# Pinning the last tiles' top-k behind the sums of the down products, and summing one-hots in one operation

## The chip, the cores and the metric

The kernel runs on one core of a Trainium2 chip. A core has engines that each work through a queue of their own in order: TensorE (PE; PEld is its loading of weights), VectorE (DVE), ScalarE (ACT), GpSimd (POOL), and SyncE (SP), which here only issues DMA transfers. The metric is the device time of one execution in microseconds (us).

## The reference

One layer over 1024 tokens of width 1024, in two halves. The first is a causal convolution beside an RWKV-7 state recurrence, then an output projection and a layer norm. The second, which the change touches, is a product-key retrieval over 128 x 128 = 16384 experts of a single neuron:

```
s1 = q[..., :128] . k1 ; s2 = q[..., 128:] . k2        # 8 heads, 128 keys each
v1, i1 = top_k(s1, 16) ; v2, i2 = top_k(s2, 16)
cand = v1[:, None] + v2[None, :]                       # 256 sums a head
sc, ci = top_k(cand, 16)
experts = i1[ci // 16] * 128 + i2[ci % 16]
gates = softmax(sc)
y2[t] = sum over k of gelu(h[t] . U[e_k]) * gate_k * V[e_k]   # 128 experts a token
x = layer_norm(alpha * x + gate2 * y2)
```

## The kernel before

The tokens are eight tiles of 128. Tiles 0 to 4 are computed densely: a matrix of gates over all 16384 experts is built for each (`gate_matrix`), and the expert stage then multiplies with all of U and V. Tiles 5 to 7 are gathered: for each of 128 choices a token, GpSimd fetches a row of U by an indirect DMA (L1098), VectorE multiplies and sums it (L1106), and then the same with V (L1113). `side` holds these three gathers one after the other, and `gather_to` takes them forward so that they end with the dense work.

The expert stage runs over 32 groups of four blocks of 128 experts. For each block the up products come first (L1178, tile `mg`, two halves of 320 tokens, 24 matmuls each, so 192 in a group). ScalarE applies gelu (L1180), VectorE multiplies with the gates (L1182), ScalarE rounds to `ah` (L1183) and VectorE takes the rest, `al` (L1184). Then come the down products (L1212, tile `md`, three banks): ten in a group, one for each tile of tokens and half of the width, 12 matmuls each. VectorE adds each to `y_acc` (L1217); in group 0 ScalarE copies it instead. The weights come as 512 KB transfers into three raw buffers, ScalarE rounds them and GpSimd takes the rest (L1143).

The choice of experts is made earlier, beside the recurrence and the projections, for tiles 0 to 5: `best16` finds the 16 largest of 128 scores or of 72 candidates, and `choose` turns their positions into two indices by one-hots (compare, L914; multiply with the indices, L917; three halvings by adds, L920; a last add, L922) and makes the softmax. There the multiply and adds are GpSimd's (`E` is `G`). For tiles 6 and 7 the scores are stored, and `choose_late` does this in the expert stage, two heads at a time, with VectorE for all of it (`E` is `V`; its tiles have names that begin with l: `lscore`, `lvi`, `lcand`, `ltkf`, `loh`). I call this the late work. Both functions are generators, and a step is what stands between two yields: 72 steps a tile. One is taken at every third step of the gathers (`LATE`).

The instructions are written in this order, and a scheduler then orders them for each engine: of those whose inputs it reckons to be ready, an engine gets the one that was written first. So an instruction that is ready early can stand well ahead of its place in the text.

Of the kernel before, what the change touches and what calls it, by code (L numbers as in the profile page):

```python
# [16 lines left out]
OP = mybir.AluOpType  # L17
AX = mybir.AxisListType
# [41 lines left out]
NPAGE = 31  # L60
TSLOW = 2
TGATE = 12
LATE = 3
CBUF = 4
GB = 3
ABUF = 6
# [13 lines left out]
def layer_kernel(ctx, tc, x, cols, c_row, cond_w, w_in, w2a2, g2, w_out, ln_rows, wq, keys, peer_u, peer_ut, peer_v, peer_vt, out):  # L80
# [785 lines left out]
    def choose(tt, val, idx, h0, nh, nb, new, E):  # L866

        n = nh * TOPK
        sh3 = [128, nh, TOPK]
        quad = lambda nm, dt=F32: new(nm, dt, 4 * n).rearrange("p (q h r) -> p q h r", q=4, h=nh)  # L870
        qf, qg, qu = quad("tkf"), quad("tkg"), quad("tku", U32)
        fp, m1, m2, m3 = (qf[:, i] for i in range(4))
        top, shf, fo = qg[:, 0], qg[:, 1], (qg[:, 2], qg[:, 3])
        pos = qu[:, 0]
        shi, qi_, ri_ = (qu[:, i].bitcast(I32) for i in (1, 2, 3))
        for hh in range(0, nh, nb):
            hs = slice(hh, hh + nb)
            cand = new("cand", F32, nb * NCAND).rearrange("p (h c) -> p h c", h=nb)
            o = 0
            for i, m, w in REGIONS:  # L880
                V.tensor_add(cand[:, :, o:o + m * w].rearrange("p h (a b) -> p h a b", b=w),
                             val[:, hs, 0, i:i + m][:, :, :, None].to_broadcast([128, nb, m, w]),
                             val[:, hs, 1, 0:w][:, :, None, :].to_broadcast([128, nb, m, w]))
                o += m * w
            for h in range(hh, hh + nb):
                best16(top[:, h], pos[:, h], cand[:, h - hh, :])
                yield

        A.activation(fp, pos, AF.Copy)
        V.tensor_scalar(m1, fp, 32.0, None, op0=OP.is_ge)  # L890
        V.tensor_scalar(m2, fp, 48.0, None, op0=OP.is_ge)
        V.tensor_scalar(m3, fp, 64.0, None, op0=OP.is_ge)
        V.tensor_add(shf, m1, m2)
        V.scalar_tensor_tensor(shf, m3, 2.0, shf, op0=OP.mult, op1=OP.add)
        V.tensor_scalar(shi, shf, -1.0, 4.0, op0=OP.mult, op1=OP.add)
        V.tensor_tensor(qi_, pos.bitcast(I32), shi, op=OP.logical_shift_right)
        V.tensor_tensor(ri_, qi_, shi, op=OP.logical_shift_left)

        V.scalar_tensor_tensor(m1, m2, 3.0, m1, op0=OP.mult, op1=OP.add)
        V.scalar_tensor_tensor(m1, m3, 24.0, m1, op0=OP.mult, op1=OP.add)  # L900
        qb = new("tkb", BF, 8 * n).rearrange("p (q h r) -> p q h r", q=8, h=nh)
        isel, jsel = qb[:, 0], qb[:, 1]
        V.scalar_tensor_tensor(isel, m1, -2.0, qi_, op0=OP.mult, op1=OP.add)
        V.tensor_sub(jsel, fp, ri_)
        yield
        put = lambda w, t: ld(sel_d[tt][w][:, h0 * TOPK:h0 * TOPK + n], t.rearrange("p h r -> p (h r)"))
        for half, sel in ((0, isel), (1, jsel)):
            ib = qb[:, 2 + half]
            A.activation(ib, idx[:, :, half, :], AF.Copy)
            for hh in range(0, nh, nb):  # L910
                hs = slice(hh, hh + nb)
                oh = new("oh", BF, nb * TOPK * TOPK).rearrange("p (h q r) -> p h q r", h=nb, q=TOPK)
                sh4 = [128, nb, TOPK, TOPK]
                V.tensor_tensor(oh, iota_q[:, None].to_broadcast(sh4), sel[:, hs, None, :].to_broadcast(sh4),  # L914
                                op=OP.is_equal)
                yield
                E.tensor_mul(oh, oh, ib[:, hs, :, None].to_broadcast(sh4))  # L917
                yield
                for w in (8, 4, 2):
                    E.tensor_add(oh[:, :, 0:w], oh[:, :, 0:w], oh[:, :, w:2 * w])  # L920
                    yield
                E.tensor_add(fo[half][:, hs], oh[:, :, 0], oh[:, :, 1])  # L922
            put(half, fo[half])
        mx = small.tile([128, NH], F32, name="mx")[:, :nh]
        V.tensor_copy(mx, top[:, :, 0])
        V.tensor_sub(top, top, mx[:, :, None].to_broadcast(sh3))
        A.activation(top, top, AF.Exp)
        sm = small.tile([128, NH], F32, name="sm")[:, :nh]
        V.tensor_reduce(sm, top, axis=AX.X, op=OP.add)
        V.reciprocal(sm, sm)  # L930
        V.tensor_mul(top, top, sm[:, :, None].to_broadcast(sh3))
        put(2, top)
        if tt in DT:
            gates.append(gate_matrix(tt))
        yield
# [187 lines left out]
    done = [0]  # L1123

    def gather_to(frac):

        while side and done[0] < frac * n_side:
            step(side)
            done[0] += 1
            if late and done[0] % LATE == 0:  # L1130
                next(late[min(late)], None)

    NBLK = [slice(a_, a_ + NW) for a_ in range(0, ND, NW)]
    NT = ND // 128
# [25 lines left out]
    for g in range(32):  # L1160
# [38 lines left out]
        for half in range(2):  # L1199
# [3 lines left out]
            for t in range(NT):  # L1203
# [10 lines left out]
                if g == 0:  # L1214
                    A.activation(ya, p, AF.Copy)
                else:
                    V.tensor_add(ya, p, ya)  # L1217
                gather_to((g + 0.5 + (NT * half + t) / (4 * NT)) / 31)
                if g == 31 and half == 1:

# [54 lines left out]
```

## Time and profile before

| | |
|---|---|
| time, median of 3 runs (lowest, highest) | 3313.77 us (3313.57, 3319.34) |
| the profiled execution | 3316.05 us, span 3314.3 us |
| TensorE busy | 3040.8 us, 92% |
| VectorE busy | 2570.2 us, 78% |
| GpSimd busy | 1838.2 us, 55% |
| ScalarE busy | 1212.7 us, 37% |
| first up product (L1178) | at 1431.5 us |
| mean granted clock of TensorE | 0.949 |

The span runs from the first to the last instruction of the profiled execution; the busy times are shares of it, averaged over stages with quite different limits. The expert stage is its second half, from 1431.5 us on. Times of instructions are from the start of the span.

### The profile page before, as it was taken

What the parts mean: (1) busy time and instruction counts of PE and PEld (TensorE: products, weight loads), DVE (VectorE), ACT (ScalarE), POOL (GpSimd) and SP (SyncE); (2) the same over time, 40 slices, a digit from 0 to 9 for tenths busy, and PEclk for the clock granted to TensorE, in tenths of its full rate; (3) what the DMA queues carried; (4) which work ended last, traced back from release to release, by engine and by line L of the source; (5) the groups of instructions that cost most, each with busy time, mean ns of one, the idle gap of its engine ahead of it and who ended that gap; (6) DMA issues with size and microseconds to landing.
All of it is one profiled execution on the core that took longest, in us unless ns stands there. A gap on an engine that the chain in (4) does not pass through costs nothing.

```text
span 3314.3 us, 54838 instructions
## 1 busy us (share of the span) xinstructions
PE 3040.8 (92%) x20400; PEld 2639.3 (80%) x20400; DVE 2570.2 (78%) x5636; ACT 1212.7 (37%) x2358; POOL 1838.2 (55%) x1448
## 2 busy tenths in 40 slices
PE   6968999999897886889899999999999999999996
PEld 4735766678786776878778899999999989898985
DVE  6389565757788889569999977777787867777877
ACT  5552443353444565643223232323232323232323
POOL 2400112233345548446676687778787868777772
PEclk9978999889799887999999999999999999999998
DMA  7885555557576876888788899999999989999994
GB/s 302 292 264 173 159 161 160 178 191 272 169 247 212 300 255 211 262 280 305 267 291 312 302 337 344 337 341 337 337 337 345 335 318 339 346 329 350 331 344 155
DMA packets 403292, 922.31 MB, mean 278 GB/s; under 512 B 80800, under 2 KB 213328, under 8 KB 381008
## 3 DMA queue, kind: packets, MB, share of 16 engines
q1 hardware_dynamic: 210192, 474.16, 41.0%
q0 software_dynamic: 110592, 402.70, 33.5%
q10 hardware_dynamic: 82240, 41.94, 4.4%
q8 instruction: 160, 2.62, 0.3%
q14 instruction: 108, 0.88, 0.1%
HBM read 788.64 MB, written 130.05 MB: 277 GB/s over the span
## 4 chain that ended last, share of the span: by engine, by line
PE 61%; DVE 25%; DMA 4%; POOL 3%; issue 3%; ACT 3%; SPq 0%; DVEq 0%; POOLq 0%; ACTq 0%
PE md L1212 21%; PE mg L1178 21%; PE mm L183 11%; DVE grow L1106 4%; DVE cacc L459 2%; PE mgate L974 2%; PE mm L467 1%; DVE cw L249 1%; DVE oa L962 1%; DVE ob L966 1%; DMA xt<-x 1%; POOL oh L920 1%; PE bank L638 1%; DVE yacc L1217 1%; DVE loh L920 1%
## 5 line engine op out<-in xcount | busy, mean ns | idle before, releaser
L1178 PE MATMUL mg<-h2h,uhi 128*128 128x320 f32 x2048 | 637.0, 311 | 12.9 <-DVE al L1184 12.9
L1178 PE MATMUL mg<-h2l,uhi 128*128 128x320 f32 x2048 | 635.6, 310 | 0.0
L1178 PE MATMUL mg<-h2h,ulo 128*128 128x320 f32 x2048 | 635.5, 310 | 0.0
L1212 PE MATMUL md<-vhi,ah 128*128 128x512 f32 x1280 | 495.2, 393 | 31.3 <-ACT ah L1183 29.0
L1113 DVE SCALAR_TENSOR_TENSOR gy<-grow,gz,gy 128x1024 f32<-128x1024 f32 x381 | 488.6, 1282 | 29.6 <-DMA grow<-peer_v,eid 27.5
L1212 PE MATMUL md<-vhi,al 128*128 128x512 f32 x1280 | 500.8, 392 | 8.2 <-DVE al L1184 8.2
L1098 POOL DMA_INDIRECT grow<-peer_u,eid x384 | 364.3, 949 | 248.7 <-DVE grow L1106 110.2
L1212 PE MATMUL md<-vlo,ah 128*128 128x512 f32 x1280 | 498.3, 391 | 0.0
L1106 DVE SCALAR_TENSOR_TENSOR grow<-grow,gh 128x1024 f32<-128x1024 f32 x384 | 460.6, 1211 | 17.8 <-DMA grow<-peer_u,eid 17.8
L1098 POOL DMA_INDIRECT grow<-peer_v,eid x384 | 361.6, 942 | 190.5 <-DVE gy L1113 106.6
L1178 PEld LDWEIGHTS mg<-h2h,uhi 128*128 128x128 f32 x2048 | 387.2, 189 | 22.8 <-DVE al L1184 17.4
L1178 PEld LDWEIGHTS mg<-h2l,uhi 128*128 128x128 f32 x2048 | 387.2, 189 | 5.1
L1178 PEld LDWEIGHTS mg<-h2h,ulo 128*128 128x128 f32 x2048 | 387.4, 189 | 3.1
L1217 DVE TENSOR_TENSOR yacc<-md,yacc 128x512 f32<-128x512 f32 x310 | 211.4, 687 | 158.0 <-PE md L1212 157.2
L1143 POOL TENSOR_TENSOR vlo<-vraw,vhi 128x1024 fp32r<-128x1024 f32 x128 | 308.9, 2413 | 27.2 <-ACT vhi L1141 24.9
L1143 POOL TENSOR_TENSOR ulo<-uraw,uhi 128x1024 fp32r<-128x1024 f32 x128 | 309.3, 2417 | 24.7 <-ACT uhi L1141 22.7
L1212 PEld LDWEIGHTS md<-vhi,ah 128*128 128x128 f32 x1280 | 240.6, 189 | 82.6 <-ACT ah L1183 33.5
L1212 PEld LDWEIGHTS md<-vhi,al 128*128 128x128 f32 x1280 | 241.5, 189 | 55.5 <-DVE al L1184 10.8
L1212 PEld LDWEIGHTS md<-vlo,ah 128*128 128x128 f32 x1280 | 241.4, 189 | 49.1
L1141 ACT ACTIVATE vhi<-vraw 128x1024 fp32r<-128x1024 f32 x128 | 135.1, 1055 | 393.5 <-DMA vraw<-peer_vt 386.1
L968 POOL TENSOR_TENSOR ob<-ob,selt 128x384 f32<-128x384 f32 x160 | 147.6, 925 | 219.7 <-DVE ob L966 154.7
L974 PE MATMUL mgate<-oa,ob 128*128 128x128 f32 x1280 | 194.4, 305 | 57.2 <-POOL ob L968 51.5
(390 smaller groups left out, 6012.9 us busy)
## 6 DMA issues: line engine op xcount, KB each, us to landing
uraw<-peer_ut SPq DMA_DIRECT2D x128, 512.0 KB, 6.7
vraw<-peer_vt SPq DMA_DIRECT2D x128, 512.0 KB, 5.6
wsplit<-split_wq SPq DMA_DIRECT2D x48, 1024.0 KB, 7.0
G_d<-stage ACTq DMA_DIRECT2D x20, 2048.0 KB, 11.2
gmat<-G_d SPq DMA_DIRECT2D x32, 1280.0 KB, 9.1
cw<-cond_w SPq DMA_DIRECT2D x48, 512.0 KB, 5.5
wsplit<-split_w_out SPq DMA_DIRECT2D x24, 1024.0 KB, 7.6
split_w_in<-wsplit SPq DMA_DIRECT2D x22, 1024.0 KB, 5.0
```

Source lines behind the costliest of these rows:

```text
L183: T.matmul(pt, l[:, k, :], r[k], start=i == 0, stop=i == 3 * KD - 1)
L459: V.scalar_tensor_tensor(a, win(i), wk(i), a, op0=OP.mult, op1=OP.add)
L968: G.tensor_mul(ob[:, :3], ob[:, :3], gt[:, ts.start:ts.start + 3, None].to_broadcast([128, 3, 128]))
L974: T.matmul(pt[:, t, :], ob[:, t, :], oa[:, t, :], start=True, stop=True)
L1098: G.indirect_dma_start(out=r, out_offset=None, in_=peer_u if k < 128 else peer_v, in_offset=bass.IndirectOffsetOnAxis(ap=eid[:, k % 128:k ...
L1106: V.scalar_tensor_tensor(r, r, 1.0, ht, op0=OP.mult, op1=OP.mult, accum_out=z[:, i:i + 1])
L1113: V.scalar_tensor_tensor(y, r, z[:, i - 128:i - 127], y, op0=OP.mult, op1=OP.add)
L1141: A.activation(hi, raw, AF.Copy)
L1143: G.tensor_sub(lo, raw, hi.bitcast(F32))
L1178: T.matmul(p, l[:, k, :], r[k][:, bs], start=i == 0, stop=i == 3 * KD - 1)
L1212: T.matmul(p, l[:, ts], r[:, e % 2, :], start=e == 0 and q == 0, stop=e == 3 and q == 2)
L1217: V.tensor_add(ya, p, ya)
```

## The change

The one-hots of the late work are summed by one reduction over a transposed view in place of four adds. `choose` gets three more yields, for all tiles. The late work is no longer advanced by the gathers' steps but by the sums of the down products from group 1 on, one step for each sum. While a step is written, each of its VectorE instructions gets an edge to that sum: VectorE's order must have it behind the sum. (Instructions of other engines get no such edge, and no wait is added, since both are on one engine.) A tile has 60 steps now.

```
-LATE = 3
...
         V.tensor_scalar(m3, fp, 64.0, None, op0=OP.is_ge)
+        yield
         V.tensor_add(shf, m1, m2)
...
         V.tensor_scalar(shi, shf, -1.0, 4.0, op0=OP.mult, op1=OP.add)
+        yield
         V.tensor_tensor(qi_, pos.bitcast(I32), shi, op=OP.logical_shift_right)
...
         V.scalar_tensor_tensor(m1, m3, 24.0, m1, op0=OP.mult, op1=OP.add)
+        yield
         qb = new("tkb", BF, 8 * n).rearrange("p (q h r) -> p q h r", q=8, h=nh)
...
                 E.tensor_mul(oh, oh, ib[:, hs, :, None].to_broadcast(sh4))
                 yield
+                if E is V:
+                    V.tensor_reduce(fo[half][:, hs], oh.rearrange("p h q r -> p h r q"), axis=AX.X, op=OP.add)
+                    continue
                 for w in (8, 4, 2):
...
             done[0] += 1
-            if late and done[0] % LATE == 0:
-                next(late[min(late)], None)
...
-                    V.tensor_add(ya, p, ya)
+                    ins = V.tensor_add(ya, p, ya)
+                    if late:
+
+                        with tc.issue_after(ins.ins):
+                            t_ = min(late)
+                            if next(late[t_], late) is late:
+                                late.pop(t_)
```

Two places in VectorE's order. The first is the start of the expert stage; `mg<-mg,gmat` is the multiply by the gates. Before:

```order
L751 MAX lvi<-lscore 128x8 x4
L752 MAX_INDEX lvi<-lvi,lscore 128x8 x4
L881 TENSOR_TENSOR lcand<-lvi 128x2x16 x2
L753 MATCH_REPLACE lscore<-lvi,lscore 128x128 x4
L754 MAX lvi<-lscore 128x8 x4
L755 MAX_INDEX lvi<-lvi,lscore 128x8 x3
L881 TENSOR_TENSOR lcand<-lvi 128x2x8
L755 MAX_INDEX lvi<-lvi,lscore 128x8
L1182 TENSOR_TENSOR mg<-mg,gmat 128x320 x3
```

The same place in the changed kernel (its line numbers are 3 to 5 higher here: L1111 is the gathers' L1106, L1185 the multiply, L1187 `al`):

```order
L1091 SCALAR_TENSOR_TENSOR eid<-gsel_14669,gsel_14671 128x128
L1111 SCALAR_TENSOR_TENSOR grow,gz<-grow,gh 128x1024 x5
L1185 TENSOR_TENSOR mg<-mg,gmat 128x320 x3
L1187 TENSOR_TENSOR al<-mg,ah 128x320 x3
L1111 SCALAR_TENSOR_TENSOR grow,gz<-grow,gh 128x1024 x2
```

The first scores' top-k stood ahead of the first multiply; now five gathers do.

The second place is one-hots of tile 6, in the middle of the up products of an early group. Before:

```order
L914 TENSOR_TENSOR loh<-iota_q,ltkb 128x512
L1106 SCALAR_TENSOR_TENSOR grow,gz<-grow,gh 128x1024 x2
L917 TENSOR_TENSOR loh<-loh,ltkb 128x512
L1184 TENSOR_TENSOR al<-mg,ah 128x320
L1106 SCALAR_TENSOR_TENSOR grow,gz<-grow,gh 128x1024
L1182 TENSOR_TENSOR mg<-mg,gmat 128x320
L920 TENSOR_TENSOR loh<-loh 128x2x128
L1106 SCALAR_TENSOR_TENSOR grow,gz<-grow,gh 128x1024
L1182 TENSOR_TENSOR mg<-mg,gmat 128x320
L920 TENSOR_TENSOR loh<-loh 128x2x64
L1184 TENSOR_TENSOR al<-mg,ah 128x320
```

One-hots of tile 6 in the changed kernel (L1220 is the sum of a down product, L916 the compare, L919 the multiply, L922 the reduction):

```order
L1220 TENSOR_TENSOR yacc<-md,yacc 128x512
L916 TENSOR_TENSOR loh<-iota_q,ltkb 128x512
L1220 TENSOR_TENSOR yacc<-md,yacc 128x512
L919 TENSOR_TENSOR loh<-loh,ltkb 128x512
L1111 SCALAR_TENSOR_TENSOR grow,gz<-grow,gh 128x1024 x2
L1220 TENSOR_TENSOR yacc<-md,yacc 128x512
L922 TENSOR_REDUCE ltkg<-loh 128x32
L1111 SCALAR_TENSOR_TENSOR grow,gz<-grow,gh 128x1024
L916 TENSOR_TENSOR loh<-iota_q,ltkb 128x512
```

They stood among the multiplies and `al` of the up products; now each step stands behind a sum, and in this group no late instruction stands between multiplies and `al`.

## Rows read from the trace of the kernel before

**Rows 1.** VectorE's busy share (tenths) in 40 slices of the span, from the page.

```profile
DVE  6389565757788889569999977777787867777877
```

**Rows 2.** Stretches of the expert stage: length, busy us (instructions) of PE PEld DVE ACT POOL, PEclk, DMA, GB/s.

```profile
1431.53:1485.76 54.23, 41.60 (x262) 39.71 (x261) 36.69 (x127) 19.28 (x32) 24.65 (x19) 0.87 0.80 279
1485.76:1931.10 445.34, 407.39 (x2192) 361.92 (x2191) 436.85 (x1026) 131.79 (x225) 302.50 (x231) 0.98 0.85 297
1986.53:2541.33 554.80, 554.80 (x3124) 507.05 (x3122) 432.68 (x650) 152.39 (x247) 427.59 (x328) 1.00 0.93 339
```

**Rows 3.** The same for the up products (L1178): PE, then PEld.

```profile
1485.76:1931.10 445.34, 215.72 (x1344) 207.49 (x1344) 0.98 0.85 297
1986.53:2541.33 554.80, 289.99 (x1921) 285.28 (x1920) 1.00 0.93 339
```

**Rows 4.** Who TensorE waited for, groups 1 to 7: us in total, times, longest.

```profile
PE md L1212 <- ACT ah L1183: 15.0, 10, 3.0
PE mg L1178 <- DVE al L1184: 12.9, 10, 2.5
```

**Rows 5.** Groups 0 to 7, VectorE's lines L1106, L1113, L1182, L1184, L1217, in this order.

```profile
1431.53:1931.10 499.57, 155.14 (x256) 0.97 0.84 295
1431.53:1931.10 499.57, 68.53 (x54) 0.97 0.84 295
1431.53:1931.10 499.57, 31.08 (x64) 0.97 0.84 295
1431.53:1931.10 499.57, 30.56 (x64) 0.97 0.84 295
1431.53:1931.10 499.57, 41.97 (x62) 0.97 0.84 295
```

**Rows 6.** VectorE in time, 1458 us: start us, us, instruction.

```profile
1458.19 1.27 DVE L1182 TENSOR_TENSOR mg<-mg,gmat 128x320 f32<-128x320 f32 x3
```

**Rows 7.** Late lines, groups 0 to 7, by shape: busy us, mean ns | idle before.

```profile
L920 DVE TENSOR_TENSOR loh<-loh 128x256 bf16<-128x256 bf16 x16 | 9.4, 590 | 0.0
L920 DVE TENSOR_TENSOR loh<-loh 128x128 bf16<-128x128 bf16 x16 | 11.8, 736 | 0.0
L920 DVE TENSOR_TENSOR loh<-loh 128x64 bf16<-128x64 bf16 x16 | 9.2, 577 | 0.1
L922 DVE TENSOR_TENSOR ltkg<-loh 128x32 f32<-128x32 bf16 x16 | 4.8, 297 | 0.1
L925 DVE COPY mx<-ltkg 128x2 f32<-128x2 f32 x8 | 10.4, 1295 | 0.0
L929 DVE TENSOR_REDUCE sm<-ltkg 128x2 f32<-128x32 f32 x8 | 1.4, 177 | 0.5 <-ACT ltkg L927 0.5
```

**Rows 8.** A reduction of 512 values elsewhere in the kernel, same view.

```profile
L713 DVE TENSOR_REDUCE gs<-yt 128x8 f32<-128x512 f32 x8 | 5.4, 674 | 0.0
```

**Rows 9.** VectorE in time, 1607 us.

```profile
1607.48 2.77 DVE L914 TENSOR_TENSOR loh<-iota_q,ltkb 128x512 bf16<-128x512 bf16 x1
```

**Rows 10.** GpSimd in time, 1607 us.

```profile
1607.54 2.43 POOL L1143 TENSOR_TENSOR ulo<-uraw,uhi 128x1024 fp32r<-128x1024 f32 x1
```

**Rows 11.** GpSimd's subtractions (L1143) in two stretches: length, POOL busy.

```profile
1485.76:1931.10 445.34, 137.80 (x58) 0.98 0.85 297
1986.53:2541.33 554.80, 193.57 (x81) 1.00 0.93 339
```

**Rows 12.** Who SyncE's queue waited for, 1450 to 1900 us.

```profile
SPq L906 <- DVE ltkg L922: 70.1, 12, 11.9
```

**Rows 13.** GpSimd in time, the fifth gather.

```profile
1452.35 0.94 POOL L1098 DMA_INDIRECT grow<-peer_u,eid  x1 [0.30 <-issue]
```

**Rows 14.** DMA issues, 1446 to 1463 us: count, median us to landing.

```profile
grow<-peer_u,eid POOLq DMA_INDIRECT x6, 10.3
```

**Rows 15.** The stretch before the expert stage, columns as in rows 2.

```profile
815.00:1431.53 616.53, 519.00 (x4767) 479.03 (x4765) 486.15 (x1621) 327.14 (x779) 312.52 (x316) 0.90 0.72 239
```

**Rows 16.** The down products (L1212) of groups 9 to 18: PE, then PEld.

```profile
1986.53:2541.33 554.80, 281.76 (x1203) 223.71 (x1202) 1.00 0.93 339
```

## Prediction

> **What bounds the kernel now.** I read the table of 40 slices first. VectorE's digits [rows 1] are 9 in the slices just after the middle, where the expert stage begins, and 7 and 8 from there on: the engine is full for some 450 us and then no longer. Next came the table by stretches, cut at the first up product of groups 0, 1, 8, 9 and 19 of the 32 groups [rows 2]. That these cuts hold whole groups is seen from the up products alone [rows 3]: 1344 are 7 x 192, and 1920 are 10 x 192. So groups 1 to 7 take 445.3 us, 63.6 each, and groups 9 to 18 take 554.8 us, 55.5 each. In the second stretch TensorE is busy for all of it, VectorE for 432.7 us (43.3 a group), and nothing waits. In the first VectorE is busy for 436.9 of 445.3 us (98.1%) while TensorE stands for 38 us. Had the first seven groups run at 55.5 they would take 388.4; the excess is 57.0 us. It is more than the 38 us of standing still: the granted clock is 0.98 on average there, that is the upper of its two levels (2.4 GHz) but for short pieces at the lower (1.2 GHz) after TensorE stood, against 1.00, and ends of matmuls are modelled.
>
> The longest waits of TensorE in those groups [rows 4] are for the copy ah, which follows VectorE's multiply by the gates (15.0 us), and for VectorE's own al (12.9). So in groups 1 to 7 VectorE is the bound, and TensorE from group 9 on. What the first has and the second has not are the late steps, the top-k and choice of tiles 6 and 7. In the 500 us of groups 0 to 7 VectorE is busy 36.7 + 436.9 = 473.5 us [rows 2]; the gathers' two lines, the multiply, al and the sums are 155.1 + 68.5 + 31.1 + 30.6 + 42.0 = 327.3 [rows 5]. The rest, 146 us, is late work, and more than that, since an instruction starts before its predecessor ends: three multiplies back to back took 1.27 us [rows 6], three single ones would be 3 x 0.486 = 1.46, so 0.09 less for each that follows. With half of the 500 instructions so packed that is 22 us, and late work 168. Between 146 and 168 I take 160, the nearer to full packing, since the engine hardly stood.
>
> **The change, part by part.** *The one-hot sums.* Three halvings and a last add, 64 instructions in all, go; their busy times are 11.8 + 9.4 + 9.2 + 4.8 = 35.2 us [rows 7]. Sixteen reductions come, 512 bf16 values each. The trace has reductions of 512 f32 values at 674 ns [rows 8]; 16 x 0.674 = 10.8 us. The difference is 24.4, less 2 for 48 packed starts: 22 us saved. The bounds: a reduction in strides of bf16 is not shown. At the least it costs what 32 elements cost, 0.18 us [rows 7], and saves 30; at the most what the four adds cost, 2.2 us, and saves nothing. I take 674 ns, the row with the same count.
>
> Why adds of 64 elements take 577 ns is seen in a pair of rows: a compare on VectorE ran from 1607.48 for 2.77 us, just behind GpSimd's subtraction of the low weights, 1607.54 for 2.43 us [rows 9, 10]. The copy of 2 elements takes 1295 ns on average for the same reason, while the small reductions stay at 177 ns [rows 7]. The Trainium skill says in "GPSIMD Engine Reference", Key points, that GpSimd's SBUF interfaces are shared with VectorE instructions that have two SBUF inputs or run in a two-port mode; a reduction is neither, so by that page the 16 never wait and 10.8 us stands, where being held as the copy is, some 1.1 us each, would make it 29. The trace agrees as far as those eight small reductions go.
>
> Against this change speaks "VectorE: DVE Perf Modes" of the Trainium skill, Rules for kernel authors: it calls `tensor_reduce` the slowest operation of VectorE, to be restructured on a hot path, and its tier table gives 16-bit adds twice the rate. By it the swap saves nothing; that is the second rival below, worked out there from rows.
>
> *The other late work* keeps its instructions. The subtractions that hold it fill 137.8 of 445.3 us now (31%) and 193.6 of 554.8 (35%) where groups are short [rows 11], so what is held grows by about an eighth. With some 55 us of the late work held, a third of it, that is +7; the bounds are 0 and +12. Late work after the change: 160 - 22 + 7 = 145 us.
>
> *The pinning.* A tile now has 4 x 15 = 60 steps and one call that finds the end, so two tiles take 122 sums, ten in each group from group 1 on: 12.2 groups, where before they were done by group 7 and partly in group 0. Each group carries 145 / 12.2 = 11.9 us. VectorE then needs 43.3 + 11.9 = 55.2 us, about TensorE's 55.5. With the 98.1% to which it was filled before, that is 56.2 a group, 0.7 over, or 9 us in all. Two engines that are both full also make each other wait. No stretch shows such a balance; bounds are 0 and 2 us a group, I take 0.6, 7 us.
>
> The pinned instructions stand behind a sum that itself waits for TensorE, and behind them on VectorE are the next gather and the next sum. Between the multiplies and al no late operation is left, as the order shows; those are what TensorE waited for [rows 4]. The steps' transfers move with them: 24 stores of the choice and 8 loads of scores go through SyncE's queue among the weights' loads. Before, SyncE stood 70 us behind the one-hot sums for such stores [rows 12], and yet none of TensorE's waits is for weights. So I cost this at nothing; the cover is the three raw buffers, and if it is gone weights come late in each group. The engines hold copies and exponentials as before.
>
> *The start.* The first multiply ran at 1458.19 [rows 6]. In the new order five gathers stand ahead of it instead of late work. The fifth of them was issued at 1452.35 [rows 13] and landing takes 10.3 us [rows 14], so it is there at about 1463 and worked off at about 1464. That is 6 us later; some of it lies beside what group 0 has to do anyway. Bounds 0 and 6, I take 4.
>
> *The middle.* Three more yields in `choose` also delay the choices of tiles 0 to 5, by three steps of the slow list each. The order there changes widely but not the work: behind the last state pass stand 496 matmuls of gate matrices instead of 492. The stretch takes 616.5 us with TensorE busy for 519.0 [rows 15]; of those 97 us of gaps a reshuffle may win or lose perhaps a tenth. I take 0, bounds 10 either way.
>
> Sum: -57 + 9 + 7 + 4 = -37 us. The profiled execution took 3316.05 us (span 3314.3 and 1.8 around it), so 3279; the median of the three runs is 2.3 lower, so 3277 for a timed run.
>
> **The rivals.**
> *TensorE alone decides.* Held work shrinks because pinned operations stand together, late work is 146 - 22 = 124 us, 10.2 a group, and VectorE needs 53.5. Then nothing is over 55.5: -57 + 0 to 6, that is 3257 to 3263. For it: one held start per cluster. Against: gathers still stand between the steps' parts.
>
> *The reduction saves nothing.* It runs as slowly as the four adds. Late work 167, 13.7 a group, 57.0 needed, 58.1 at 98.1%: 2.6 x 12.2 = 32, with 7 and 4 -14 in all: 3302, timed 3300. For it: strides of bf16 that no row shows; against it the 674 ns.
>
> *The down products' part is too short for it.* All ten steps now fall in the half of a group with the sums. There VectorE has ten sums of 0.68 (6.8 us), 11.9 of late work and, by the order, eleven gathers of 1.21 (13.3): 32.0 us. TensorE's down products take 281.8 / 10 = 28.2 us [rows 16]. The 3.8 us are made up in the other half only if sums may lag: there are three banks, so two tiles of 2.8 us, 5.6. If they may not, 12.2 x 3.8 = 46 comes back: -57 + 46 + 4 = -7, 3309, timed 3307, hardly a change. With dear reductions too the half needs 33.8, 5.6 a group is missing, which is all the lag there is, and 68 comes back: +15, 3331, timed 3329, slower than before. It decides from 57 / 12.2 = 4.7 us a group on. For it: the late work is no longer spread over both halves. Against: the order has gathers in the other half to give way, and the lag covers 3.8.
>
> **How the numbers follow.** My forecast (3266 to 3290) has 0.48; TensorE alone (up to 3266) 0.18; the reduction that saves nothing, or waits of 2 us a group (3290 to 3306) 0.18; the short half without lag (3307 to 3320) 0.08; slower 0.08. About 0.2%, 6.6 us, is what a measurement tells from no change. So faster 0.84, same 0.08, slower 0.08. The range takes in the second and third: 3257 to 3306.
>
> **What would show it.** Groups 1 to 7 at 56 to 57.5 us instead of 63.6, and late instructions on VectorE as far as group 12 or 13; 16 reductions of 0.6 to 0.7 us, unheld; TensorE's waits on ah and al below 15 us in groups 1 to 12; the first multiply some 5 us later than 1458 counted from the first up product. I am wrong if the groups up to 12 stay above 59 us, if waits for sums (the md banks) take the place of those for ah and al, or if the stage begins more than 10 us before or after 1431.5.

## The result, and the profile after

The changed kernel takes 3289.64 us (median of 5 runs, 3284.70 to 3293.64), the kernel before in the same comparison 3313.77 (5 runs, 3302.12 to 3321.13): a ratio of 0.9918, 95% interval 0.9902 to 0.9935 (the two medians alone give 0.9927). By the medians that is 24 us faster where 37 were forecast. The profiled execution took 3292.2 us, span 3290.4. Later, on another chip, the changed kernel had 3291.43 us (6 runs) with 0.9927 (0.9906 to 0.9948).

First the table by stretches of the changed kernel, as [rows 2]: length, busy us (instructions) of PE, PEld, DVE, ACT, POOL, then PEclk, DMA share, GB/s. Cut at the first up product of groups 0, 1, 15 and 25, since late work now reaches group 14.

```profile
1431.89:1489.90 58.01, 43.33 (x268) 41.56 (x267) 26.09 (x49) 19.28 (x32) 33.10 (x26) 0.85 0.88 317
1489.90:2297.35 807.45, 790.05 (x4373) 718.47 (x4371) 726.89 (x1526) 240.61 (x400) 596.71 (x456) 0.99 0.91 326
2297.35:2852.00 554.65, 552.87 (x3114) 505.05 (x3113) 429.40 (x635) 151.84 (x247) 427.10 (x326) 1.00 0.93 336
```

The same for the up products (now L1181), as [rows 3], to show whole groups:

```profile
1489.90:2297.35 807.45, 420.79 (x2689) 410.43 (x2688) 0.99 0.91 326
2297.35:2852.00 554.65, 290.27 (x1920) 285.37 (x1919) 1.00 0.93 336
```

The weight loads count 2688 = 14 x 192 and 1919, one record short of 10 x 192. So groups 15 to 24 take 55.5 us each, the pace of [rows 2], and groups 1 to 14 take 57.7. Below, *excess* is what groups 1 to 14 take over 14 x 55.48 = 776.7 us: 30.7 here. Before, the same 14 groups have 56.4, 57.0 of it in groups 1 to 7, where now 13.8 are left. With -25.7 for the excess, +3.8 for group 0 and +0.4 for the start of the stage (1431.89 against 1431.53), 21.5 of the span's 23.9 us are found; the rest lies behind group 14.

TensorE's waits in groups 1 to 14, the answer to [rows 4] (us in total, times, longest):

```profile
PE mg L1181 <- DVE al L1187: 14.5, 9, 3.9
PE md L1215 <- ACT ah L1186: 2.8, 3, 1.2
```

TensorE stands for 17.4 us of the 807.45, and its busy time is 790.05 us against 776.7 at the pace, so the other 13.3 us of the excess are busy time. Most of that is the granted clock: it is 0.50 (1.2 GHz) for 24 us in all in these groups, each time beside a standstill, and 1.00 (2.4 GHz) otherwise. As an estimate, 24 us at half the clock lose some 12.

VectorE is still what TensorE waits for. But VectorE is not full: 726.89 of 807.45 us, 90.0%, where it was 98.1% in [rows 2]. Groups 1 and 14 bear on that mean, since they carry only 1.7 and 2.8 us of late work; the other twelve carry about 11.5 us each, and there VectorE is busy for 91.9%. The mean is no ceiling either. The same columns for groups 2 to 13, for group 7 (the longest), for group 8 behind it, and for a piece of group 7:

```profile
1545.54:2241.24 695.70, 678.30 (x3745) 616.38 (x3744) 639.60 (x1364) 202.85 (x340) 507.49 (x386) 0.98 0.90 322
1828.75:1892.03 63.28, 59.36 (x318) 53.80 (x316) 55.52 (x87) 18.65 (x29) 45.83 (x35) 0.95 0.89 315
1892.03:1948.16 56.13, 55.71 (x313) 50.62 (x312) 55.09 (x113) 15.04 (x27) 42.70 (x34) 1.00 0.91 334
1867.20:1874.00 6.80, 5.44 (x20) 5.45 (x21) 6.80 (x11) 4.86 (x8) 4.59 (x5) 0.50 0.81 277
```

Group 8 keeps nearly to the pace with VectorE busy for 98.1% of it, and group 7 takes 63.3 us with 87.7% (62.8 us and 88.7% in a second profile of this kernel, told of below). So 55 us of VectorE's time cost next to nothing in one group and 8 us in the other: it matters when each piece is done, not only how much there is. In group 7 VectorE stood first for a row of a gather, with sums and late steps behind it in its order. The sums ran late, and late steps pinned to them came to stand between a gelu and its multiply by the gates. Here is that piece of time, cut (start us, us, instruction, idle before):

```profile
1839.01 1.29 DVE L1118 SCALAR_TENSOR_TENSOR gy<-grow,gz,gy 128x1024 f32<-128x1024 f32 x1 [3.58 <-DMA grow<-peer_v,eid]
...
1857.88 0.42 ACT L1183 ACTIVATE mg<-mg 128x320 f32<-128x320 f32 x1
1858.86 0.68 DVE L919 TENSOR_TENSOR loh<-loh,ltkb 128x512 bf16<-128x512 bf16 x1
1859.46 0.68 DVE L1220 TENSOR_TENSOR yacc<-md,yacc 128x512 f32<-128x512 f32 x1
...
1861.38 1.14 DVE L922 TENSOR_REDUCE ltkg<-loh 128x32 f32<-128x512 bf16 x1
1862.44 2.73 DVE L931 TENSOR_TENSOR ltkg<-ltkg,mx 128x32 f32<-128x32 f32 x1
1865.09 1.28 DVE L1118 SCALAR_TENSOR_TENSOR gy<-grow,gz,gy 128x1024 f32<-128x1024 f32 x1
1866.28 0.48 DVE L1185 TENSOR_TENSOR mg<-mg,gmat 128x320 f32<-128x320 f32 x1
...
1868.56 0.64 PE L1181 MATMUL mg<-h2h,uhi 128*128 128x320 f32 x1 [3.85 <-DVE al L1187]
```

The gelu (L1183) of the multiply at 1866.28 had ended 8 us before it. TensorE then stood for the al that follows that multiply: 3.85 us, its longest wait.

The view that I had not read is who VectorE itself waited for. Before, groups 1 to 7:

```profile
DVE mg L1182 <- ACT mg L1180: 3.5, 4, 1.2
DVE al L1184 <- ACT ah L1183: 1.7, 3, 0.8
DVE grow L1106 <- DMA grow<-peer_u,eid: 1.2, 1, 1.2
DVE yacc L1217 <- PE md L1212: 0.9, 2, 0.7
```

And after, groups 1 to 14:

```profile
DVE mg L1185 <- ACT mg L1183: 18.5, 23, 5.2
DVE grow L1111 <- DMA grow<-peer_u,eid: 12.2, 9, 3.2
DVE gy L1118 <- DMA grow<-peer_v,eid: 11.5, 9, 3.6
DVE al L1187 <- ACT ah L1186: 10.2, 11, 2.7
DVE yacc L1220 <- PE md L1215: 7.5, 10, 1.9
DVE al L1187 <- ACT vhi L1144: 6.5, 3, 3.2
```

Seven us of waiting in 445 have become 66 in 807. The waits are of the kind there always is in this stage: gelu on ScalarE, rows of a gather that have not landed, the copy ah, a down product. Before, a late instruction could stand in VectorE's order wherever such a wait would have been; pinned behind the sums it cannot. (A wait of VectorE costs time only where TensorE in turn waits for it, so the 66 us are not a price: in the lightest kernel below VectorE stands for 91 of 778 us and hardly anything is lost.)

The late lines by shape, groups 1 to 14, as [rows 7] (busy us, mean ns | idle before):

```profile
L922 DVE TENSOR_REDUCE ltkg<-loh 128x32 f32<-128x512 bf16 x16 | 18.2, 1135 | 0.0
L916 DVE TENSOR_TENSOR loh<-iota_q,ltkb 128x512 bf16<-128x512 bf16 x16 | 16.9, 1054 | 0.1
L919 DVE TENSOR_TENSOR loh<-loh,ltkb 128x512 bf16<-128x512 bf16 x16 | 13.2, 826 | 0.0
L930 DVE COPY mx<-ltkg 128x2 f32<-128x2 f32 x8 | 4.4, 554 | 0.0
```

and the first two of these with the least, median and longest duration (ns):

```profile
L916 DVE TENSOR_TENSOR loh<-iota_q,ltkb x16: 415/420/3204, 1599.7 to 2211.1; 128x512 bf16<-128x512 bf16 x16
L922 DVE TENSOR_REDUCE ltkg<-loh x16: 1104/1128/1182, 1606.3 to 2242.7; 128x32 f32<-128x512 bf16 x16
```

A compare of 0.42 us is held up to 3.2; no reduction is held at all. But a reduction takes 1.13 us, not the 0.67 of [rows 8].

### The profile page after: what moved, and what is told of

Its sections match the earlier page's. It is cut to its first block, busy times and chain, and to the rows that moved or that the text cites. A ratio compares the mean times of both kernels' runs of the same rounds, so it can differ in the third digit from the quotient of the medians.

```text
span 3290.4 us, 54741 instructions
## 1 busy us (share of the span) xinstructions
PE 3042.0 (92%) x20400; PEld 2646.7 (80%) x20400; DVE 2548.7 (77%) x5588; ACT 1213.5 (37%) x2358; POOL 1842.6 (56%) x1448
## 4 chain that ended last, share of the span: by engine, by line
PE 61%; DVE 21%; DMA 9%; issue 4%; ACT 3%; POOL 2%; SPq 1%; DVEq 0%; POOLq 0%; ACTq 0%
PE mg L1181 21%; PE md L1215 19%; PE mm L182 11%; DMA G_d<-stage 2%; DVE cacc L458 2%; DVE grow L1111 2%; PE mgate L979 2%; DMA grow<-peer_v,eid 1%; PE mm L466 1%; DVE yacc L1220 1%; DVE gy L1118 1%; DVE cw L248 1%; DMA xt<-x 1%; DVE oa L967 1%; DMA grow<-peer_u,eid 1%
## 5 line engine op out<-in xcount | busy, mean ns | idle before, releaser
L1181 PE MATMUL mg<-h2h,uhi 128*128 128x320 f32 x2048 | 639.0, 312 | 14.5 <-DVE al L1187 14.5
L1181 PE MATMUL mg<-h2l,uhi 128*128 128x320 f32 x2048 | 637.4, 311 | 0.0
L1181 PE MATMUL mg<-h2h,ulo 128*128 128x320 f32 x2048 | 637.0, 311 | 0.0
L1118 DVE SCALAR_TENSOR_TENSOR gy<-grow,gz,gy 128x1024 f32<-128x1024 f32 x381 | 488.1, 1281 | 28.3 <-DMA grow<-peer_v,eid 23.2
L1111 DVE SCALAR_TENSOR_TENSOR grow<-grow,gh 128x1024 f32<-128x1024 f32 x384 | 461.2, 1212 | 50.1 <-DMA grow<-peer_u,eid 38.0
L1181 PEld LDWEIGHTS mg<-h2h,uhi 128*128 128x128 f32 x2048 | 389.2, 190 | 23.8 <-DVE al L1187 18.4
L1181 PEld LDWEIGHTS mg<-h2l,uhi 128*128 128x128 f32 x2048 | 389.1, 190 | 4.9
L1181 PEld LDWEIGHTS mg<-h2h,ulo 128*128 128x128 f32 x2048 | 388.9, 190 | 2.6
L1220 DVE TENSOR_TENSOR yacc<-md,yacc 128x512 f32<-128x512 f32 x310 | 211.4, 685 | 122.9 <-PE md L1215 113.3
```

Of the source, the lines that this page charges most:

```text
L1111: V.scalar_tensor_tensor(r, r, 1.0, ht, op0=OP.mult, op1=OP.mult, accum_out=z[:, i:i + 1])
L1118: V.scalar_tensor_tensor(y, r, z[:, i - 128:i - 127], y, op0=OP.mult, op1=OP.add)
L1181: T.matmul(p, l[:, k, :], r[k][:, bs], start=i == 0, stop=i == 3 * KD - 1)
L1220: ins = V.tensor_add(ya, p, ya)
```

## The experiments

"Late work" in the table is VectorE's time in late instructions in groups 1 to 14, each counted from its start or its predecessor's end, whichever is later; "share" is VectorE's busy share in those groups. These three and the excess are of the one profiled run; times are medians of all runs, from which a profiled run lies up to 12 us away. Ratios are against the kernel before on the same chip. In the kernel before and the first experiment late work is done by group 7 or 8, and part of it in group 0, so their shares are over stretches of two kinds.

| kernel | late work | share | excess | time | ratio (95%) |
|---|---|---|---|---|---|
| before | 149.2 | | 56.4 | 3311.5 to 3319.6 | |
| reduction alone | 131.5 | 88.5% | 39.6 | 3308.13 | 0.9979 (0.9967, 0.9992) |
| pins alone | 161.3 | 90.7% | 39.4 | 3299.82 | 0.9951 (0.9933, 0.9969) |
| casts on VectorE | 156.7 | 90.4% | 37.7 | 3295.85 | 0.9940 (0.9920, 0.9961) |
| changed kernel | 142.9 | 90.0% | 30.7 | 3289.64 | 0.9918 (0.9902, 0.9935) |
| changed kernel again | 145.6 | 90.9% | 22.4 | 3291.43 | 0.9927 (0.9906, 0.9948) |
| both halves | 177.4 | 93.6% | 31.0 | 3283.58 | 0.9906 (0.9886, 0.9926) |
| no gathers emitted early | 143.0 | 90.5% | 24.1 | 3287.69 | 0.9910 (0.9886, 0.9935) |
| contiguous, twice | 142.2 | 89.8% | 26.2 | 3284.63 | 0.9903 (0.9882, 0.9924) |
| contiguous reduction | 135.8 | 90.7% | 12.2 | 3268.97 | 0.9859 (0.9831, 0.9888) |
| two of three | 115.2 | 88.2% | 12.8 | 3270.22 | 0.9862 (0.9839, 0.9885) |
| two of three, contiguous, casts | 110.9 | 88.7% | 3.8 | 3263.35 | 0.9837 (0.9814, 0.9860) |
| two of three, contiguous | 103.1 | 88.3% | 1.6 | 3264.33 | 0.9845 (0.9824, 0.9866) |

**The noise first.** The changed kernel was run again beside the last two others.

> The changed kernel once more, beside the two others on the same chip, to see how far the excess of groups 1 to 14 (30.7 us) and the start of the first group (1431.9 us) move between two profiles of one program. Both theories: 3286 to 3296, excess 27 to 35 us, start within 2 us. If the start or the excess moves by 5 us or more, differences of that size between the other experiments tell nothing.

The time came as expected, but the excess moved by 8.3 us between two profiles of one program, and the stage began 2.8 us earlier. The second profile is of a run of 3279.21 us, the first of one of 3292.2. In the second TensorE stands for 13.9 us in groups 1 to 14, not 17.4, and has the lower clock for 14 us, not 24: some 5 of the 8.3 us are the clock's, an estimate at half speed. So a difference of 8 us in one profile's excess tells nothing by itself, and neither do 3 us in the start.

**The parts.** First the reduction in the kernel before:

```diff
                 yield
+                if E is V:
+                    V.tensor_reduce(fo[half][:, hs], oh.rearrange("p h q r -> p h r q"), axis=AX.X, op=OP.add)
+                    continue
                 for w in (8, 4, 2):
```

> The kernel before with the one-hots of the late work summed by one reduction, and nothing else: steps at every third gather step, no pinning, no new yields. Theory: in groups 1 to 7 VectorE is the bound, so what it is spared comes off the time. The 64 adds took 35.2 us; the reduction of the changed kernel was seen at 1.13 us, 16 of them 18 us: 17 us less, so about 3297 us, and groups 1 to 7 some 17 us shorter together. Rival: the time for which the adds were held by GpSimd's subtractions only passes on to the next late operation: then hardly 5 us, 3308 us or more.

Its excess fell by 16.8 us, as much as VectorE's late work (17.7), but the timed median fell less: by 6.5 us against the 3314.6 of that comparison, to 3308.13. That is where the rival had put it. The profiled run took 3301.54 us, so profile and median do not agree on the size. In groups 1 to 6 of this kernel, whose late work is not pinned, VectorE is busy for 99.5% of the time. Then the pins and yields, with the four additions in place of the reduction, in one step:

```diff
                 if E is V:
-                    V.tensor_reduce(fo[half][:, hs], oh.rearrange("p h q r -> p h r q"), axis=AX.X, op=OP.add)
+                    for w in (8, 4, 2):
+                        V.tensor_add(oh[:, :, 0:w], oh[:, :, 0:w], oh[:, :, w:2 * w])
+                    V.tensor_add(fo[half][:, hs], oh[:, :, 0], oh[:, :, 1])
                     continue
```

> The changed kernel with the four adds back in place of the reduction, in the same step, so that the number of steps and their places stay. Theory: VectorE is nearly full in groups 1 to 13, and 17 us more late work (35.2 us of adds for 18 of reductions) come on top of the time: about 3306 us. Rival: pinned adds stand together and are held but once, a little over 0.8 us a one-hot, less than the reduction's 1.13: then no change or a gain of some 5 us, 3285 to 3290 us.

The pins alone bring 15 us, with more late work than before (161.3 us); the time lies between the two forecasts. By the times 6.5 and 14.8 make 21, near the 24 and 20 of the whole change. By the excess each part alone takes off 17 us, and both together 26 to 34, but a single profile is good to 8 us only. Neither part is idle.

**Load or place?** Two late steps behind three sums:

```diff
-                    if late:
+                    sums[0] += 1
+                    if late and sums[0] % 3:
```

> The changed kernel with a late step behind two of three sums in place of each: 6.7 steps a group, done by group 19 instead of 13. Theory of the load (VectorE needs 43 + 12 of 55.5 us a group, and two nearly full engines wait for each other) and theory of the short half (ten sums, ten steps and eleven gathers do not fit the 28 us of the down products) both say: 7.8 us of late work a group leave room, and the 31 us by which groups 1 to 14 exceed 55.5 a group fall to 8 or less: about 3267 us. Rival, ScalarE's queue: gelu stands behind late conversions and exponentials that wait for pinned steps; their number stays, so the excess stays near 25 us, 3283 us or more.

Five of ten steps behind the sums, five behind al in the other half (`late_step` holds the pinning of the changed kernel):

```diff
-                V.tensor_sub(al[:, bs], p, ah[:, bs].bitcast(F32))
+                ins = V.tensor_sub(al[:, bs], p, ah[:, bs].bitcast(F32))
+                if g > 0 and (bs.start > 0 or e == 0):
+                    late_step(ins)
...
-                    if late:
+                    if t % 2 == half:
+                        late_step(ins)
```

> The changed kernel with ten steps a group as before, but five of them pinned behind sums and five behind al of the up products. The load of a group is the same, only the half differs. Theory of the short half: the excess of 31 us falls to some 10 us, about 3269 us. Theory of the load: it stays, 3285 to 3293 us. If the steps between multiplies and al hurt as they did in the kernel before, it is slower than the changed kernel, 3295 us or more.

A lighter group cures most of it: 12.8 us are left, nearly all in two groups. Spreading over both halves does not: VectorE is filled to 93.6%, but the same late instructions take 177 us instead of 143 (the compare 1281 ns on average, the multiply 1060), and the excess is the same. So the edit did not keep the load, as it was meant to, and does not decide on the short half: what a second half may have given back, held work may have taken. That steps behind late sums do run into the up products is seen in group 7 above.

**ScalarE's queue.** In the longest group of two of three (65.0 us) ScalarE stands for 17.6 us at a late cast, with a weight's rounding and a gelu behind it:

```profile
2064.88 0.23 ACT L911 ACTIVATE ltkb<-lvi 128x32 bf16<-128x32 uint32 x1 [17.63 <-DVE lvi L754]
2065.02 1.04 ACT L1144 ACTIVATE vhi<-vraw 128x1024 fp32r<-128x1024 f32 x1
2065.97 0.42 ACT L1183 ACTIVATE mg<-mg 128x320 f32<-128x320 f32 x1
```

That gelu had its products at 2060.7, so it stood some 5 us behind the cast. The casts are not pinned, and ScalarE works in order, as these rows show. I took that for the cause of what is left, and moved them:

```diff
-        A.activation(fp, pos, AF.Copy)
+        V.tensor_copy(fp, pos) if E is V else A.activation(fp, pos, AF.Copy)
...
-            A.activation(ib, idx[:, :, half, :], AF.Copy)
+            V.tensor_copy(ib, idx[:, :, half, :]) if E is V else A.activation(ib, idx[:, :, half, :], AF.Copy)
...
+        if E is V:
+            yield
         A.activation(top, top, AF.Exp)
...
-                A.activation(ah[:, bs], p, AF.Copy)
+                act = A.activation(ah[:, bs], p, AF.Copy)
...
-                        with tc.issue_after(ins.ins):
+                        with tc.issue_after(ins.ins), tc.issue_after(act.ins):
```

> The changed kernel with ScalarE relieved of what waits for pinned VectorE steps: the position cast and the index cast of the late work run on VectorE, and the late Exp is issued one step after the subtraction that feeds it and pinned on ScalarE behind the last cast ah. Same number of steps behind the sums, so the same load on VectorE (about 1.2 us more in all).
> Theory 1 (what remains in the changed kernel, 30.7 us over the even pace in groups 1 to 14, is mostly ScalarE's queue: late casts and Exp waiting for VectorE with a gelu behind them): the excess of groups 1 to 14 falls to 10 to 18 us, the waits of ScalarE at those casts (40.7 and 28.8 us) are gone and the wait at Exp (48.5 us) is under 10; time 3274 to 3280.
> Theory 2 (VectorE simply is too full with a late step behind every sum): the excess stays at 28 to 34 us, time 3287 to 3292.

The 69.5 us of waits at the casts went (that at Exp stayed, 44.4 us), and the excess did not fall: 37.7. The casts cost VectorE 10.8 us, not the 1.2 that I had put down, since they are held too. So relief of ScalarE and 14 us more late work came together, and this run alone does not part them. The opposite test is two of three with the contiguous reduction and the casts left on ScalarE:

> Two late steps in three sums and the contiguous reduction, with the late casts and Exp as the changed kernel has them on ScalarE (the seventh experiment without its relief of ScalarE's queue). Theory 1 (VectorE's load alone): late work in groups 1 to 14 is about 105 to 110 us, the excess is 0 to 5 us as in the seventh experiment, time 3258 to 3266. Theory 2 (a cast on ScalarE that waits for a pinned step holds a gelu, as it looked in groups 9 and 11 of the third experiment, and that costs even where VectorE has room): excess 8 to 13 us, time 3266 to 3273.

Its ScalarE still waits for late VectorE steps (groups 1 to 14; us, times, longest):

```profile
ACT ltkb L911 <- DVE lvi L754: 30.7, 8, 11.8
ACT ltkf L888 <- DVE ltku L754: 30.1, 6, 7.3
ACT ltkg L938 <- DVE ltkg L937: 19.0, 4, 8.4
```

and its TensorE waits for nothing worth naming:

```profile
PE md L1221 <- ACT ah L1192: 0.5, 1, 0.5
PE mg L1187 <- DVE al L1193: 0.3, 1, 0.3
PE md L1221 <- DVE yacc L1226: 0.2, 1, 0.2
```

So 80 us of ScalarE's waiting cost nothing where VectorE has room: there the waits are VectorE's lateness seen through ScalarE. What they cost in the changed kernel, where VectorE is fuller, no run isolates.

**The reduction's stride.** Late one-hots laid out with the summed index innermost:

```diff
+                if E is V:
+                    V.tensor_tensor(oh, iota[:, None, None, :TOPK].to_broadcast(sh4),
+                                    sel[:, hs, :, None].to_broadcast(sh4), op=OP.is_equal)
+                    yield
+                    V.tensor_mul(oh, oh, ib[:, hs, None, :].to_broadcast(sh4))
+                    yield
+                    V.tensor_reduce(fo[half][:, hs], oh, axis=AX.X, op=OP.add)
+                    continue
```

> The changed kernel with the late one-hots laid out with the summed index innermost, so that the reduction reads 512 bf16 in a row, and not at 32-byte strides; compare and multiply read other broadcasts. Theory 1 (the stride is why the reduction takes 1.13 us): it takes 0.66 to 0.70 us as the contiguous f32 reduction of 512 elements does, VectorE has some 7 us less in groups 1 to 14, and 3 to 7 of them show: 3283 to 3287. Theory 2 (bf16 input or the 32 sums make it dear): still 1.05 to 1.15 us, time 3287 to 3292, equal to the changed kernel.

Its late lines:

```profile
L917 DVE TENSOR_TENSOR loh<-iota,ltkb 128x512 bf16<-128x512 f32 x16 | 18.4, 1151 | 0.1
L922 DVE TENSOR_REDUCE ltkg<-loh 128x32 f32<-128x512 bf16 x16 | 10.8, 672 | 0.0
L920 DVE TENSOR_TENSOR loh<-loh,ltkb 128x512 bf16<-128x512 bf16 x16 | 10.0, 626 | 0.0
```

The duration is the stride's doing: 0.67 us, as forecast for it. (The compare now reads f32, and its median rose from 0.42 to 0.68 us, but the multiply's fell from 0.68 to 0.41.) But from 7.1 us less late work the excess fell by 10 to 18.5 us, by which profile of the changed kernel one takes, and the time by some 20 us, more than either theory had. TensorE stands for 7.1 us and has the lower clock for 3.4. Was it the work, or that the longest unheld late instruction had gone? Each reduction was done twice, so the work is that of the changed kernel again, in short pieces:

```diff
                     V.tensor_reduce(fo[half][:, hs], oh, axis=AX.X, op=OP.add)
+                    V.tensor_reduce(fo[half][:, hs], oh, axis=AX.X, op=OP.add)
```

> The sixth experiment (contiguous reduction) with each late reduction done twice, the second over the first: 16 more instructions of 0.67 us, 10.8 us, which bring the late work of that kernel (135.8 us) to 146 to 147 us, about that of the changed kernel (142.9), but in short instructions. Theory 1 (the sum of VectorE's work decides, since it carries no more than about 700 us in the 777 us of 14 groups at TensorE's pace): the excess of groups 1 to 14 rises from 12.2 to 21 to 32 us and the time from 3269 to 3279 to 3290. Theory 2 (the 1.13 us reduction hurt by its length, since one long instruction ahead of a multiply is waited for): excess 10 to 16, time 3267 to 3274.

With 142.2 us of late work the excess is 26.2, between the changed kernel's two, and the time 3284.6. So it was the amount, as theory 1 had it, and not the length of an instruction.

**The first group.** No gather steps emitted behind the up products of group 0:

```diff
-            gather_to((g + e / 8) / 31)
+            if g:
+                gather_to((g + e / 8) / 31)
```

> The changed kernel without gather steps behind the up products of the first group; the steps left out are caught up behind its down products. If gathers ahead of the first multiply make the first group longer (58.0 us against 54.2 before), it falls to 54 to 55 us and the time by 3 to 4 us, to 3285 to 3287. If the first group is long for the wait of its down products on ah (14.7 us) alone, whatever VectorE does, it stays at 57 to 59 and the time at 3288 to 3292. If the caught-up steps hold the sums of the down products instead, group 0 or 1 gets longer by more than it gained.

Group 0 stayed at 58.1 us, but this does not decide: in its trace five gathers still stand ahead of the first multiply (at 1460.02), since the scheduler put the steps from behind the down products there. The edit did not do what I wanted, and the price of those gathers was not isolated.

**Both together.** Two of three, the contiguous reduction and the moved casts:

> Two late steps in three sums (as in the third experiment), with the relief of ScalarE's queue and the contiguous reduction. If ScalarE's queue is what was left of that experiment's excess (12.8 us in groups 1 to 14, in groups 9 and 11), the excess falls to 0 to 4 us and the time to 3255 to 3262. If a gather's transfer and VectorE's load made those two groups long, the excess stays at 10 to 15 us and the time at 3266 to 3273.

The excess is 3.8 us and the time 3263.35. By the run without the casts (3264.33, excess 1.6) that gain is the load's, not ScalarE's. Groups 1 to 14 of that run, columns as above, and then those of two of three:

```profile
1491.28:2269.56 778.28, 777.23 (x4369) 709.11 (x4368) 687.40 (x1372) 232.05 (x386) 598.46 (x457) 1.00 0.92 338
```

```profile
1486.19:2275.73 789.54, 781.11 (x4370) 711.60 (x4369) 696.40 (x1369) 230.80 (x386) 597.99 (x457) 1.00 0.92 333
```

In the first TensorE is busy for 777.23 of 778.28 us, and the granted clock is 1.00 throughout. The two versions with two of three and a contiguous reduction are faster than the kernel before by 47 to 56 us and than the changed one by some 26.

## Why the prediction was right, and where its size was off

*The number.* The range held, but the forecast's own part of it (3266 to 3290) by 0.4 us, and the repeat (3291.43) lies in the next part, that of a reduction that saves nothing or of waits of 2 us a group. The second of these two is what came: the excess is 2.2 and 1.6 us a group. Of the signs that it named, groups 1 to 7 take 57.4 us each as forecast (56 to 57.5), and TensorE's waits for sums did not take the place of the others. The waits on ah and al are 17.3 us, a little over the 15; late work goes on to group 14, not 12 or 13; and the reductions are not of 0.6 to 0.7 us.

*What bounds the kernel.* Right. The excess belongs to VectorE's late work, and a version with less of it per group has none.

*The first seven groups give back 57.0 us.* Right in kind: they keep 13.8 us of excess because late work now runs there too, but with less of it in each group.

*The sums of one-hots, 22 us saved with 674 ns each.* Too much: 16 reductions take 18.2 us, so the 35.2 of [rows 7] fall by 17.0, not 24.4. I took the duration of a contiguous f32 row for a strided bf16 one. That they are never held is right: 1104 to 1182 ns for all sixteen, while compares beside them reach 3204. This is what "GPSIMD Engine Reference" of the Trainium skill, Key points, gives for an instruction with one input outside the two-port modes, and the trace agrees.

*The rule against it*, that a reduction is the slowest operation ("VectorE: DVE Perf Modes" of the Trainium skill, Rules for kernel authors), did not decide: 1.13 us for each reduction against 2.2 us for the four adds as [rows 7] has them, most of which were held. The medians of the four make 0.88 us, so unheld they would beat the strided reduction: what it saves it saves by never being held. In the kernel with pins alone the four still took 35.9 us in all. That its 16-bit type brings a reduction nothing, as the page's table has it, agrees: 672 ns for 512 contiguous bf16, 674 for 512 f32 in [rows 8].

*Held work +7, late work 145 us in all.* The total is right, 142.9 and 145.6 us, but by luck, since three errors cancel. Counted as in the table, the late work before was 172 us, group 0 with it, not 160. The sums of one-hots saved 14 of them, not 22. And the other late work fell by 13 to 16 us where it was to grow by 7. The multiply's mean fell to 826 ns and the copy's from 1295 in [rows 7] to 554.

*The pinning, 9 us for what is over the pace and 7 us for mutual waits.* This is the term that was mis-sized: 16 forecast, 30.7 and 22.4 measured. The load was not the error. Late instructions run from group 1 to group 14, but the first and the last of these carry little, so it is twelve groups with about 11.5 us each, where 12.2 with 11.9 were forecast. VectorE's other work there is 41.8 us, where 43.3 were forecast. By the prediction's own rule 53.3 us of work at 98.1% need 54.3 us, and nothing would be over the pace of 55.5. So the first of the two terms should have been nothing, and the whole excess belongs to the second, "Two engines that are both full also make each other wait". It was taken at 0.6 us a group; over these twelve groups it was 2.5 and 1.8 us, about the upper bound of 2. What failed is "With the 98.1% to which it was filled before". In groups 2 to 13 of the six kernels with ten steps a group, all behind sums, VectorE is busy for 91.9 to 93.0% (in the two profiles of the changed kernel for 91.9 and 93.0). In the three kernels with two steps behind three sums it is 90%, but there VectorE has less to do and TensorE sets the pace nearly everywhere, so that is no limit. Nor are 92 or 93% a limit: they are the mean of groups that in the changed kernel range from 88 to 98%. The term also had nothing in it for TensorE's clock, which by the estimate above took some 12 and 7 us of the excess.

Why the share fell has two readings, and no run parts them. One is the pins: loose late work can stand in VectorE's order wherever an instruction would wait, and work pinned behind a sum cannot; nor can it keep clear of the up products once the sums run late, as in group 7. For this speaks that the reduction alone, the same late operations without pins, has 99.5% in groups 1 to 6. The other is the load: there, and in the kernel before, VectorE has some 21 us of late work a group, more than fits beside TensorE's pace, so it always has something to do; in every kernel with ten pinned steps the load is near the pace, and two nearly even queues wait for each other in turn. For this speaks that steps in both halves, with 14 us of late work a group, have 96.3%. Loose late work thinned to 11.5 us a group was not run; it would decide. What is shown is that the excess follows VectorE's late work in a group: with less of it, 12.2 and then 1.6 us are left.

*The start, +4.* Measured +3.8, and the five gathers can be read, waits first for rows to land, then the multiply 2.4 us later than in [rows 6], counted from the first up product. TensorE's wait for ah in group 0 grew from 12.2 to 14.7 us and the granted clock there fell from 0.87 to 0.85; what the gathers alone cost was not isolated.

```profile
1450.96 1.22 DVE L1111 SCALAR_TENSOR_TENSOR grow<-grow,gh 128x1024 f32<-128x1024 f32 x1 [6.49 <-DMA grow<-peer_u,eid]
...
1459.86 1.22 DVE L1111 SCALAR_TENSOR_TENSOR grow<-grow,gh 128x1024 f32<-128x1024 f32 x1 [2.74 <-DMA grow<-peer_u,eid]
...
1461.00 1.29 DVE L1185 TENSOR_TENSOR mg<-mg,gmat 128x320 f32<-128x320 f32 x3
```

*The middle at nothing* and *SyncE's queue at nothing*: the stage starts 0.4 us later, and no wait of TensorE in groups 1 to 14 is for weights. SyncE's stand at the stores of the choice fell from the 70.1 us of [rows 12]:

```profile
SPq L908 <- DVE ltkg L922: 39.8, 10, 12.8
```

*The rivals.* "TensorE alone decides" did not happen, though its 3257 to 3263 is where two of three with a contiguous reduction arrives (3264). "The reduction saves nothing" was wrong: the kernel with pins alone takes 10 us more than the changed one. The short half was neither shown nor ruled out: the edit that was to test it raised the held work.

## What to carry to other kernels

An engine's fill in a stretch that has more work than time, in loose pieces, is no capacity for a stretch whose load is near the pace and whose pieces are pinned: there the waits come back. A forecast should take the fill of a stretch that is like the new one in load and order (here 92 to 93%), or leave that much room. Count load per period, not in all: the same late work, thinned from ten steps a group to between six and seven and with its reductions made contiguous, cost almost nothing over 19 groups, where over 14 it cost 22 to 31 us. Where TensorE stands, count the clock as well: by the estimate above, the time at the lower clock cost half to two thirds as much again as the standstills beside it. And a wait that ends on one engine (ScalarE's casts) may only pass on another's lateness; the test is a kernel in which the wait stays and the load goes.

## What the runs showed of the hardware

A VectorE reduction of 512 bf16 into 32 sums took 1.13 us when its summed elements lay 32 bytes apart, and 0.67 us when they lay in a row. VectorE's small casts of 32 elements took 462 and 419 ns on average beside GpSimd's subtractions (2.42 us each). TensorE's clock was granted at 0.50 for 24 us in groups 1 to 14 of one profile of the changed kernel and for 14 us in the other, each time beside a standstill, and for none of them in the kernel in which TensorE stood for only 1 us. Two profiles of one program so differed by 8 us in the excess of these groups.
